# Four norms between sublayers: the second 1/RMS applied to the products' results instead of their operand

## The chip, the cores and the metric

The kernel runs on one core of a Trainium2 chip. The metric is the device time of one execution in microseconds: the median of several runs. A profile of one execution shows what each engine did: TensorE (PE, with its weight loads as PEld), VectorE (DVE), ScalarE (ACT), GpSimd (POOL) and SyncE (SP), which here only issues the weights' DMAs.

## The reference, cut to what matters

Two blocks of a hybrid model over 256 tokens and 16 learned ones (T = 272), width 1024. In the first block two layers follow each other, a gated delta rule and an mLSTM, each with a convolving FFN behind it, and a norm on both sides of every sublayer ("sandwich"):

```python
for i in range(DEPTH):                      # 2 layers
    a_in = rms_norm(hs, norm_w[i, 0])
    mix = gated_deltanet(a_in, ...) if i % 2 == 0 else mlstm(a_in, ...)
    hs = hs + keep * rms_norm(mix, norm_w[i, 1])
    f = conv_ffn(rms_norm(hs, norm_w[i, 2]), ...)
    hs = hs + keep * rms_norm(f, norm_w[i, 3])
...
# conv_ffn: u = causal_depthwise_conv(h @ w_up, conv_w) + conv_b
#           (silu(u[..., :2816]) * u[..., 2816:]) @ w_down
x = x + 0.5 * swiglu(rmsnorm(x, ffn1_norm), ffn1_w_gu, ffn1_w_down)   # second block begins
```

So a sublayer's result goes through one norm (first 1/RMS) into the residual, and the new residual through another (second 1/RMS) into the next sublayer's first products. This happens four times: delta rule to FFN, FFN to mLSTM, mLSTM to FFN, FFN to the second block's SwiGLU.

## The kernel before

**Operands.** Activations lie with features on the partitions, 8 tiles of 128 features by T, S + 2 = 258 or S = 256 tokens. Every product is made in three passes of fp32r: activations and weights are split into a high part (ScalarE's copy) and a low part (source minus high part, on VectorE or GpSimd), and TensorE adds high*high, low*high and high*low. `wload` (line 356) brings a block of at most 1024 weight values a partition (512 KB) by a DMA on SP's queue, three buffers deep, and makes its high part (`wh`) on ScalarE and its low part (`wl`) on VectorE, or in two pieces on GpSimd. Which of the two is set by tables: `POOL_FIRST` (0, 4, 2, 2, 0, 0, 0) is how many loads behind each norm go to GpSimd first, `POOL_EVERY` (0, 0, 0, 2, 4, 0, 4) says that later every so many do. Both are indexed by `seg`, which counts norms.

**Products.** `linears_g` makes the first two products behind a norm together (gate and up, or q and k, 256 columns each), operand tile by operand tile as these come; its four results take three of the ring's buffers in PSUM and the bank pc2. `linear_g` makes 256 columns: two result tiles in two of three PSUM buffers. `conv_ffn` has eleven blocks of 256 gate and 256 up columns; for each result its `conv` takes one ScalarE step and two VectorE steps that read PSUM. `swiglu_up` has eleven blocks without a convolution.

**The norm.** While the last products of a sublayer run, `mix_tile` takes each result tile: ScalarE squares it (`macc`), multiplies it by the norm's weight into `mw` and squares that (`mwacc`), VectorE multiplies `mw` by the residual (`mcross`). TensorE adds these over the partitions (`early` the first parts, `colsum_end` the last). `mix_end` works out the first 1/RMS `r`, and from the three sums the new residual's sum of squares `c` and the second 1/RMS `r2`. The residual's update, mw times r and hst plus mw, runs on GpSimd; then, for each operand tile, VectorE makes y = residual * weight * r2 (`xn`), ScalarE the high part, VectorE the low part (`xhl`). At T = 272 `warm` gives TensorE some products whose result nobody reads while it waits.

**Order.** One pass over the program writes the instructions; `Threads` interleaves generators (the main thread, the mLSTM's gates and heads, the memory's products) into one fixed order of TensorE's queue by an estimate of all engines' times. Within `manual_schedule` VectorE and GpSimd run in the order of the text. Behind the second norm `ml_gates` multiplies 8 gate columns, turns the result to tokens on the partitions and works out running sums that all four heads wait for. `add_tile` adds the SwiGLU's result to the residual (`ps * 0.5 + x`), and `prenorm` is the fifth norm, which this change doesn't restructure; between these the memory's products fill TensorE's waits.

## Time and profile before

| | us |
|---|---|
| median of 3 runs | 1698.15 (1695.23 to 1698.38) |
| span of the profiled execution | 1697.1 |
| TensorE busy | 1568.4 (92%) |
| VectorE busy | 1096.0 (65%) |
| ScalarE busy | 924.7 (54%) |
| GpSimd busy | 633.7 (37%) |

The profile comes from one execution. The share of busy time is a mean over stages with different limits; what a stage is worth is read from its own stretch. In a timeline a line gives start, length, engine, operation and tiles, and in brackets how long the engine sat idle before it and what ended that.

### The profile page before, as it was taken

How to read it: one execution, taken by the hardware profiler on the slowest of the kernel's cores; microseconds unless marked ns; L12 is line 12 of the kernel's file. 1: busy time of each engine (PE TensorE's matmuls, PEld its weight loads, DVE VectorE, ACT ScalarE, POOL GpSimd, SP SyncE). 2: the span in 40 equal slices, each digit the busy share in tenths (PEclk: the TensorE clock that was granted, in tenths of full speed). 3: DMA queues.
4: the chain of work that ended last, by engine and by line, in shares of the span. 5: the costliest groups of instructions: out<-in, count | busy, mean ns of one | idle time of the engine just before them, and what ended most of it. 6: DMA issues, size and time to landing. Idle time of an engine off the chain costs nothing.

```text
span 1697.1 us, 31097 instructions
## 1 busy us (share of the span) xinstructions
PE 1568.4 (92%) x11949; PEld 1475.9 (87%) x11949; DVE 1096.0 (65%) x2118; ACT 924.7 (54%) x1877; POOL 633.7 (37%) x585
## 2 busy tenths in 40 slices
PE   7888888899799997999799998999997999999999
PEld 5778787799799996888799997999986789989987
DVE  3888877767788757357777667545459563465543
ACT  3567767655466553446466555544444664554442
POOL 3675554330500004551544443212265548512221
PEclk7999999999999999899999998999998999999999
DMA  4322221226355552345366553656554335546564
GB/s 120 105 83 62 76 63 51 76 88 214 91 179 169 171 177 76 103 112 161 100 184 188 180 173 120 199 171 195 172 168 125 114 92 155 177 148 186 181 192 149
DMA packets 238570, 235.45 MB, mean 139 GB/s; under 512 B 11254, under 2 KB 226054, under 8 KB 238422
## 3 DMA queue, kind: packets, MB, share of 16 engines
q1 hardware_dynamic: 237318, 230.87, 45.4%
q0 software_dynamic: 832, 2.28, 0.5%
q8 instruction: 94, 1.54, 0.4%
q14 instruction: 54, 0.44, 0.1%
q10 hardware_dynamic: 272, 0.31, 0.1%
HBM read 232.39 MB, written 1.05 MB: 138 GB/s over the span
## 4 chain that ended last, share of the span: by engine, by line
PE 67%; DVE 22%; ACT 5%; DMA 3%; issue 2%; POOL 1%; ACTq 0%; DVEq 0%; POOLq 0%
PE ps L191 52%; PE pst L191 4%; DVE rq_a L191 3%; DVE cy L191 3%; DVE RT L191 2%; ACT wh L191 2%; DVE rq_y L191 1%; DVE wl L191 1%; POOL wl L378 1%; DMA wraw<-in_ffn_w_up_dram 1%; DVE xhl L191 1%; PE xp L191 1%; DVE xn L191 1%; DVE fy L191 1%; DVE on L191 1%
## 5 line engine op out<-in xcount | busy, mean ns | idle before, releaser
L191 PE MATMUL ps<-xhl,wh 128*128 128x256 f32 (+2 forms) x4624 | 882.0, 293 | 31.9 <-ACT xhl L191 17.3
L191 PEld LDWEIGHTS ps<-xhl,wh 128*128 128x128 f32 x4624 | 721.1, 192 | 42.5 <-ACT xhl L191 19.4
L191 ACT CAST wh<-wraw 128x1024 fp32r<-128x1024 f32 (+2 forms) x436 | 447.8, 1029 | 391.7 <-PE ps L191 263.7
L191 PE MATMUL ps<-xhl,wl 128*128 128x256 f32 (+2 forms) x2312 | 644.3, 288 | 0.8 <-DVE wl L191 0.8
L378 POOL TENSOR_TENSOR wl<-wraw,wh 128x512 fp32r<-128x512 f32 (+3 forms) x264 | 334.3, 1290 | 533.2 <-ACT wh L191 508.9
L191 PEld LDWEIGHTS ps<-xhl,wl 128*128 128x128 f32 x2312 | 435.8, 193 | 1.4 <-DVE wl L191 1.0
L191 DVE TENSOR_TENSOR wl<-wraw,wh 128x1024 fp32r<-128x1024 f32 (+3 forms) x234 | 285.0, 1219 | 210.4 <-ACT wh L191 205.1
L191 POOL TENSOR_TENSOR wl<-wraw,wh 128x512 fp32r<-128x512 f32 (+1 forms) x140 | 180.2, 1309 | 150.6 <-ACT wh L191 138.1
L191 PE MATMUL ps<-hh,wh 128*128 128x256 f32 (+1 forms) x1056 | 191.2, 283 | 0.0
L191 PEld LDWEIGHTS ps<-hh,wh 128*128 128x128 f32 x1056 | 163.4, 189 | 0.0
L191 PE MATMUL ps<-hh,wl 128*128 128x256 f32 (+1 forms) x528 | 149.8, 284 | 0.0
L191 DVE SCALAR_TENSOR_TENSOR fy<-ps,pvt,fy 128x256 f32<-128x256 f32 (+2 forms) x176 | 84.9, 487 | 25.0 <-ACT fy L191 23.1
L191 PEld LDWEIGHTS ps<-hh,wl 128*128 128x128 f32 x528 | 99.7, 189 | 0.0
L191 DVE SCALAR_TENSOR_TENSOR cy<-cx,pvt,cy 128x271 f32<-128x271 f32 (+2 forms) x96 | 73.9, 772 | 9.8 <-ACT cy L191 8.7
L191 DVE TENSOR_TENSOR hh<-fy,hh 128x256 fp32r<-128x256 f32 (+1 forms) x88 | 65.0, 741 | 13.1 <-ACT hh L191 12.8
L191 POOL MEMSET mvt<- 128x4 f32 x4 | 0.4, 102 | 177.2 <-PE ps L191 177.2
L299 POOL TENSOR_TENSOR mw<-mw,rstd 128x544 f32<-128x544 f32 (+5 forms) x20 | 24.1, 1206 | 111.4 <-ACT rstd L191 111.4
L191 ACT ACTIVATE fy<-ps,pvt 128x272 f32<-128x272 f32 (+1 forms) x88 | 49.6, 568 | 11.9 <-PE ps L191 11.3
L191 PE MATMUL pst<-wh,hh 128*128 128x512 f32 x176 | 55.0, 394 | 0.0
L191 ACT CAST hh<-fy 128x256 fp32r<-128x256 f32 (+1 forms) x88 | 35.6, 407 | 30.3 <-DVE fy L191 29.7
L191 DVE CAST_PREDICATED RT<-lvl,w 128x512 f16<-128x512 uint8 x67 | 44.9, 682 | 6.0 <-PE w L191 5.3
L191 PE MATMUL ps<-og,wh 128*128 128x272 f32 x256 | 48.6, 289 | 0.2 <-DVE og L191 0.2
(511 smaller groups left out, 2369.8 us busy)
## 6 DMA issues: line engine op xcount, KB each, us to landing
wraw<-in_ffn_w_up_dram SPq DMA_DIRECT2D x88, 512.0 KB
wraw<-in_ffn_w_gu_dram SPq DMA_DIRECT2D x88, 512.0 KB
wraw<-in_ffn_w_down_dram SPq DMA_DIRECT2D x79, 512.0 KB
wraw<-in_gdn_w_in_dram SPq DMA_DIRECT2D x48, 512.0 KB
wraw<-in_w_in_dram SPq DMA_DIRECT2D x41, 512.0 KB
wraw<-in_ml_w_in_dram SPq DMA_DIRECT2D x24, 512.0 KB
wraw<-in_gdn_w_out_dram SPq DMA_DIRECT2D x16, 512.0 KB
wraw<-in_ml_w_out_dram SPq DMA_DIRECT2D x8, 512.0 KB
```

The costliest lines, as they stand in the source:

```text
L191: r = f(*args, **kw)
L299: (eng or self.V).tensor_tensor(out, a, b, op)
L378: eng.tensor_tensor(l[:, a, b], r[:, a, b], h[:, a, b].bitcast(F32), ALU.subtract)
```

## The change

Behind the four norms the residual's update moves from GpSimd to VectorE. As soon as a residual tile is updated, its product with the norm's weight, not yet times r2, is split into high and low part (`raw`), and the first products take it. The sum of squares and r2 are worked out in between and behind; r2 is kept as `self.r` and multiplies results:

- `conv_ffn`: for the first three of eleven blocks every result is multiplied by r2 into SBUF (`scaled`) ahead of the convolution. Meanwhile `scaled_operand` makes the operand as before, a few tiles behind each product; the other blocks take it.
- `mlstm`: q and k of the first two heads and v of heads 0 and 1 take r2 when they leave PSUM, on VectorE instead of ScalarE; the gates take it by tokens, for which r2 is transposed.
- the second block's SwiGLU: the gate's results are scaled in all eleven blocks, and the factor of up is applied behind the down product, in `add_tile`, as two steps.

Further: of the early sums only `macc`'s remains early; the late weight's low part is set to VectorE; `warm` runs five products once instead of two and seven. Comments and docstrings are taken out too.

```diff
@@ mix_tile
-            self.th.add([self.early([self.macc, self.mwacc, self.mcross], N)])
+            self.th.add([self.early([self.macc], N)])
@@ mix_end
         pm = yield from self.colsum_end(0, self.macc[1])
-        pb = yield from self.colsum_end(1, self.mwacc[1])
-        pa = yield from self.colsum_end(2, self.mcross[1])
+        pb = yield from self.colsum(self.mwacc, N, "pc1")
+        yield ["pc2"]
+        pa = yield from self.colsum(self.mcross, N, "pc2")
...
-            self.rstd(r2[:], c, D, NW[1])
-            for k in range(0, KD, 2):
-                y = [self.sm(N, "xn", "y") for _ in range(2)]
-                for n in range(2):
-                    self.stt(y[n][:], src[k + n], self.pv(wcol + k + n), r2[:], ALU.mult, ALU.mult)
-                    self.A.copy(X[k + n][0], y[n][:])
-                for n in range(2):
-                    self.tt(X[k + n][1], y[n][:], X[k + n][0].bitcast(F32), ALU.subtract)
...
+                self.tt(w, w, r[:, None, :].to_broadcast([128, n, N]), ALU.mult)
+                if k == 1:
+                    self.tt(u[:], pb[:], r[:], ALU.mult)
+                    self.stt(u[:], pa[:], 2.0, u[:], ALU.mult, ALU.add)
+                self.tt(s2, s2, w, ALU.add)
+                for j in range(k, k + n):
+                    h, l = raw[j]
+                    wc = self.pv(wcol + j)
+                    self.act(h, src[j], AF.Copy, scale=wc)
+                    self.stt(l, src[j], wc, h.bitcast(F32), ALU.mult, ALU.subtract)
                 if k == 2:
+                    self.prefetch(loads[late:], low, self.V)
                     for f in low:
                         f()
+                    self.tt(u[:], u[:], r[:], ALU.mult)
+                    self.tt(c, u[:], c, ALU.add)
+            self.near_load = self.nload + POOL_FIRST[self.seg]
+            self.rstd(r2[:], c, D, NW[1])
+        return raw, self.scaled_operand(src, wcol, N) if full else None
+
+    def scaled_operand(self, src, wcol, N):
+        X = []
+        for k, (h, l) in enumerate(self.xslots(N)):
+            y = self.sm(N, "xn", "y")
+            self.stt(y[:], src[k], self.pv(wcol + k), self.r[:], ALU.mult, ALU.mult)
+            self.split(h, l, y[:])
+            X.append((h, l))
+            yield X
+
+    def scaled(self, p, N):
+        y = self.sm(N, "py")
+        self.tt(y[:], p, self.r[:], ALU.mult)
+        return y[:]
@@ conv_ffn
-                y = conv(p, 2 * c + m)
+                y = conv(self.scaled(p, N) if c < 3 else p, 2 * c + m)
...
-                yield from self.linear_g(W, c * 256, 256, KD, X, N, gate)
-                yield from self.linear_g(W, FF + c * 256, 256, KD, X, N, up)
+                for c0, fn in ((c * 256, gate), (FF + c * 256, up)):
+                    yield from self.linear_g(W, c0, 256, KD, x, N, fn)
+                    if len(X) < KD:
+                        X = next(todo) and next(todo)
@@ ml_gates
+        yield [self.r[:], "pb1"]
+        p = self.bank("pb1", (128, 3, 128), "mrp")
+        for t, (o, P) in enumerate(TT):
+            self.tr(p[:P, t, :], self.r[:, o:o + P])
+        rt = self.cst([128, 3], name="rtok", tag="rtok")
+        for t, (o, P) in enumerate(TT):
+            self.V.tensor_copy(rt[:P, t:t + 1], p[:P, t, 0:1])
...
-            self.V.tensor_copy(ga[:P, t, :], p[:P, t, :])
+            self.ts(ga[:P, t, :], p[:P, t, :], rt[:P, t:t + 1], ALU.mult)
@@ mlstm
+                elif (kind, n) in raws:
+                    self.stt(t[:, m, :], p, sc, self.r[:], ALU.mult, ALU.mult)
@@ swiglu_up
-                self.act(gs[m][:], p, AF.Silu)
+                self.act(gs[m][:], self.scaled(p, S) if late else p, AF.Silu)
@@ add_tile
-        self.stt(x, ps, scale, x, ALU.mult, ALU.add)
+        if scale == 0.5:
+            y = self.sm(S, "ady", "y")
+            self.stt(y[:], ps, scale, self.r[:], ALU.mult, ALU.mult)
+            self.tt(x, x, y[:], ALU.add)
```

## Rows read from the trace of the kernel before

**Rows 1.** The page's first lines: span, and TensorE's busy time, its share and its instructions.

```profile
span 1697.1 us, 31097 instructions
...
PE 1568.4 (92%) x11949; PEld 1475.9 (87%) x11949; DVE 1096.0 (65%) x2118; ACT 924.7 (54%) x1877; POOL 633.7 (37%) x585
```

**Rows 2.** Windows around the four norms: busy us of each engine (instructions), granted clock, DMA.

```profile
425.20:454.90 29.70, 22.45 (x129) 19.85 (x128) 21.70 (x30) 12.15 (x22) 18.38 (x15) 0.89 0.18 55
643.90:676.00 32.10, 24.11 (x142) 20.11 (x140) 23.03 (x35) 13.16 (x26) 15.49 (x13) 0.89 0.13 35
809.35:837.06 27.71, 21.27 (x126) 19.19 (x127) 19.66 (x29) 10.81 (x19) 17.06 (x15) 0.88 0.16 51
1021.24:1052.50 31.26, 24.78 (x134) 22.38 (x133) 22.04 (x41) 15.36 (x40) 16.29 (x14) 0.84 0.28 85
```

**Rows 3.** Chain of work at the first norm, 425 to 456 us: start, us, what.

```profile
427.09 0.49 ACT rstd L191
...
436.29 2.86 DVE xn L191 x2
...
440.71 6.30 PE ps L191 x38
...
449.38 1.90 DVE xhl L191 x2
```

**Rows 4.** Timeline, VectorE, 426 to 447 us: start, us, operation, [idle before it <- releaser].

```profile
428.07 0.44 DVE L191 TENSOR_TENSOR sqn<-rsp,rstd 128x272 f32<-128x272 f32 x1 [1.56 <-ACT rstd L191]
...
429.10 0.91 DVE L191 TENSOR_TENSOR sqn<-sqn,rstd 128x272 f32<-128x272 f32 x1
...
440.93 0.90 DVE L191 SCALAR_TENSOR_TENSOR xn<-hst,pvt,rstd 128x272 f32<-128x272 f32 x2
...
442.68 1.22 DVE L191 TENSOR_TENSOR wl<-wraw,wh 128x1024 fp32r<-128x1024 f32 x1
```

**Rows 5.** Timeline of the other engines at the first norm, 425 to 452 us.

```profile
426.06 0.43 ACT L191 ACTIVATE sq<-mw 128x272 f32<-128x272 f32 x1
...
426.43 1.08 PE L191 MATMUL rsp<-sq,ones 128*128 128x272 f32 x4
...
447.03 2.00 ACT L191 CAST wh<-wraw 128x1024 fp32r<-128x1024 f32 x2 [1.86 <-PE ps L191]
...
448.16 5.50 POOL L378 TENSOR_TENSOR wl<-wraw,wh 128x512 fp32r<-128x512 f32 x4 [7.80 <-ACT wh L191]
```

**Rows 6.** Tile fy, first FFN, 450 to 640 us: duration ns min/median/max.

```profile
L191 DVE SCALAR_TENSOR_TENSOR fy<-ps,pvt,fy x88: 486/496/502, 452.4 to 580.8; 128x271 f32<-128x271 f32 x44, 128x270 f32<-128x270 f32 x44
...
L191 DVE TENSOR_TENSOR fy<-fy,sg x22: 431/442/1529, 458.1 to 581.3; 128x272 f32<-128x272 f32 x22
```

**Rows 7.** Tile fy, second FFN, 830 to 1015 us.

```profile
L191 DVE SCALAR_TENSOR_TENSOR fy<-ps,pvt,fy x88: 468/479/485, 834.6 to 961.8; 128x256 f32<-128x256 f32 x88
...
L191 DVE TENSOR_TENSOR fy<-fy,sg x22: 410/738/1515, 841.3 to 962.3; 128x256 f32<-128x256 f32 x22
```

**Rows 8.** Windows: second and third 256 columns of both FFNs' up-projections.

```profile
454.90:480.10 25.20, 23.71 (x190) 23.53 (x189) 20.82 (x32) 16.67 (x28) 4.25 (x4) 1.00 0.61 187
837.10:862.00 24.90, 23.28 (x194) 23.10 (x193) 18.65 (x30) 16.27 (x28) 11.58 (x10) 1.00 0.61 188
```

**Rows 9.** Timeline behind the second norm, 666 to 690 us: the mLSTM's gates.

```profile
668.03 0.38 ACT L191 COPY gr<-psmg 8x272 f32<-8x272 f32 x1 [2.40 <-PE psmg L191]
...
669.77 0.30 DVE L191 COPY mga<-mgp 128x8 f32<-128x8 f32 x3 [3.67 <-PE mgp L191]
...
672.42 1.26 DVE L191 TENSOR_SCALAR lp_s<-lp_t 128x12 f32<-128x12 f32 x1 [1.66 <-ACT lp_t L191]
...
681.32 0.59 PE L191 MATMUL mbp<-mlf,cc 128*128 128x4 f32 x2 [5.34 <-DVE mlf L191]
```

**Rows 10.** Timeline behind the fifth norm, 1236 to 1244 us.

```profile
1236.58 0.42 DVE L191 SCALAR_TENSOR_TENSOR hst<-ps,hst 128x256 f32<-128x256 f32 x1 [5.75 <-PE ps L191]
...
1243.24 0.30 PE L191 MATMUL krp<-xhl,wh 128*32 128x256 f32 x1 [0.29 <-ACT memv L191]
```

More of the change, by code (lines that the diff above doesn't have):

```diff
@@ L353, in log1p_exp_neg_abs, with wload @@
         return p
-    def wload(self, w, k0, nk, c0, nc_, pieces=1, late=None, own=None):
+    def wload(self, w, k0, nk, c0, nc_, pieces=1, late=None, own=None, eng=None):
         key = w.tensor.name, k0, c0
@@ L679, in warm, with mix_end @@
             self.mm(p[:, :x.shape[1]], self.ones[:], x)
-    def mix_end(self, src, wcol, N, loads=(), late=1):
+    def mix_end(self, src, wcol, N, loads=(), late=1, full=True):
         late = len(loads) - late
@@ L1609, in mlstm @@
         self.lane = None
-        yield from self.linears_g([job("q", 0), job("k", 0)], KD, X, T)
+        yield from self.linears_g([job("q", 0), job("k", 0)], KD, raw, T)
+        X = next(todo) and next(todo)
         for kind, n in (("v", 0), ("v", 1), ("q", 1), ("k", 1), ("v", 2), ("v", 3), ("o", 0), ("o", 1), ("o", 2), ("o", 3)):
@@ L1615, in mlstm @@
             else:
-                yield from self.linear_g(w, c0, 256, KD, X, T, fn)
+                yield from self.linear_g(w, c0, 256, KD, raw if (kind, n) in raws else X, T, fn)
+                while len(X) < KD:
+                    next(todo)
+                    if len(X) in (5, 8):
+                        break
         return Y
@@ L1669, in first @@
         self.pause[1].set()
-        X = yield from self.mix_end(hs, PV_F1, S, self.ffn_loads(i["ffn1_w_gu_2"][0]))
+        X, _ = yield from self.mix_end(hs, PV_F1, S, self.ffn_loads(i["ffn1_w_gu_2"][0]), full=False)
         self.x2 = hs
```

67 lines of the change are left out of this document (33 added, 34 removed).

## The prediction

> **What bounds the kernel now.** I read the page's first lines, then the stretches around the norms, then the chain and the timelines inside them. TensorE is busy for 92% of the span [rows 1], so time is won only where it waits. One kind of such place is the norm behind each sublayer: from the last product of a sublayer to the end of the two products that follow (gate and up, or q and k) there pass 29.70, 32.10, 27.71 and 31.26 us, in which TensorE is busy 22.45, 24.11, 21.27 and 24.78 us, part of it at the lower clock (mean granted 0.84 to 0.89) or with work put in to fill time [rows 2]. The reader should see why it lasts in the chain of the first one [rows 3]: sums and the first 1/RMS (its Ln starts at 427.09, VectorE uses the result at 428.07 [rows 4]), then a second 1/RMS, and only at 436.29 the first scaled operand. VectorE's small steps are slow there: the operation with one operand in PSUM takes 0.44 us, the next, with both in SBUF, 0.91 [rows 4], while GpSimd updates the residual. Later the operands 6 and 7 wait behind two weight casts of 2.00 us on ScalarE [rows 5] and end at about 451.3 [rows 3].
>
> **The new way to the first products.** The first norm is worked out; the others are scaled from it.
> Sums: two of the three early sums no longer stand ahead of the one that the first 1/RMS needs. ScalarE's last own square ends at 426.49 [rows 5], and Ln started at 427.09 [rows 3]: up to 0.6 saved, so 1/RMS is usable 2.3 us behind the last product instead of 2.87.
> Operands: the second 1/RMS leaves the path; the residual's update comes onto it, from GpSimd to VectorE. A dependent VectorE step costs about 0.52 (two from 428.07 to 429.10), one that multiplies and subtracts 0.45 (0.90 for two), a weight's low part 1.22 [rows 4]. No row shows the 544-wide step on VectorE: between 0.65 (by elements from the 1.22) and 0.88 (two of 0.44), I take 0.75, near the middle, as it is as close to one bound as to the other. Operand 0: 0.52 + 0.52 + a ScalarE copy of 0.5 + 0.45 = 2.0. Operand 1 with two steps of the second sum in between: 2.9. Each of three pairs: 0.75 + 0.75 + 0.5 + 0.45 + 0.45 = 2.9, together 8.7. Between them the late weight's low part and two more steps of the sum, 2.2. Together 15.8 us.
> A new collision: TensorE has used up operands 0 to 3 while VectorE still makes 4 to 7, so the next two weights are cast then and GpSimd makes their low parts, four pieces in 5.50 us [rows 5], against VectorE. Between 0 and 5.5 us; I take 2.2, as the loop's steps that are left then are about half in number of those that GpSimd's pieces could hold.
> Behind the last operand 26 products remain at 0.125 (23.71 us for 190 [rows 8]), 3.25.
> Sum: 2.3 + 15.8 + 2.2 + 3.25 = 23.55 against 29.70, 6.1 us earlier. Third norm, 258 wide (15.0 for 15.8): 22.75 against 27.71, 5.0 earlier. Second, with 0.4 for the gates' products in between: 23.95 against 32.10, 8.1 earlier. Fourth: no GpSimd pieces (VectorE makes these low parts, behind the second 1/RMS): 2.3 + 14.9 + 1.8 + 1.2 + 2.9 = 23.1 against 31.26, 8.2 earlier; the memory's products that fill the wait now are still done beside it. TensorE starts each time some 8 us earlier than today, but VectorE paces it, so the start isn't the gain.
>
> **What takes it back behind the norms.** First and third norm (the two convolving FFNs): for three of eleven column blocks every result is first scaled by VectorE, 12 times 0.44, and the scaled operand is made after all, 8 times 0.45 + 0.43: 12.3 us more (11.8 in the second FFN). In the two blocks behind the first, VectorE is idle for 25.20 - 20.82 = 4.4 us and 24.90 - 18.65 = 6.25 us [rows 8]. It can begin on results when the second 1/RMS is done, 22.1 us into the stretch (15.8 + 2.3 + 2.2 + four steps of 0.45), at 447.3 instead of 452.4 [rows 6], 5.1 earlier; in the second FFN at 830.65 instead of 834.6 [rows 7], 4.0 earlier. Short: 12.3 - 4.4 - 5.1 = 2.8 and 11.8 - 6.25 - 4.0 = 1.55 us.
> The convolution's steps now read the scaled copy in SBUF, not PSUM. From PSUM none of the 88 took over 0.502 us, while the product with both operands in SBUF takes 0.44 in the median and up to 1.53 in the first FFN [rows 6], and 0.74 in the median in the second [rows 7], where GpSimd makes half the low parts (11.58 us busy in these two blocks, against 4.25 [rows 8]). Bounds for what this adds: nothing, or one operation held by about 1.0 us for each of GpSimd's pieces, 4 in the first FFN (two more weights behind the four pieces counted above) and 10 in the second [rows 8]. I take 2 and 4.5, half and nearly half, as the medians 0.44 and 0.74 say that holding follows GpSimd's share. Below nothing it can't be, as no SBUF operation becomes a PSUM one.
> The Trainium skill's page "SBUF — State Buffer", section "Who interferes with whom", has a rule against this edit: a VectorE instruction with two SBUF inputs contends with a GpSimd instruction that reads SBUF, one with a single SBUF input doesn't. By that rule all 24 convolution steps of the three blocks become exposed, and the sum would go to the upper bound, 14 us instead of 6.5; the trace agrees in kind (0.502 at most, against 1.53).
> TensorE bears some lateness: the last pair's convolution and products lie behind the stretch, and one result buffer in three is spare, about 24 matmuls or 2.9 us; an estimate of 4 us (0 to 6). So the first FFN ends its third block at +2.8 + 2 - 4 = 0.8 us later than today, the second at 1.55 + 4.5 - 4 = 2.0 later: the 6.1 and 5.0 are spent there.
> Second norm: TensorE stands at 676 and waits for the gates' sums until 681.32, and the steps of their chain are held by GpSimd too (1.26 us for 12 columns) [rows 9]. The gates' product ends with operand 7, some 3.5 us sooner than the 668.0 of [rows 9], but 1/RMS must be transposed and copied in the same bank (about 1.3 us), and VectorE's queue gets four result scalings and two operands (3.5 us) among the 11.5 us of steps from 669.77 to 681.3. So that wait ends between 3 us earlier and 2 later; I take 0.5 earlier. The longer chain lets the planner put some 16 products (2 us) ahead of the wait. Together 2.5 of the 8.1 stay. If that cover is not used, 0.5.
> Fourth norm: VectorE only gets 22 scalings of gate results (9 us over 130), with room; I let 8.2 stand. At the end of that FFN each of 8 tiles takes two VectorE steps instead of one of 0.42; the last is on the path to the fifth norm, where TensorE waits just 0.29 us today [rows 10] behind the memory's products: 0.4 lost.
> ScalarE's eight more copies per norm lie in its idle time (12.15 of 29.70 us busy [rows 2]); SP issues the same loads, earlier.
>
> **Sum.** 0.8 - 2.5 + 2.0 - 8.2 + 0.4 = -7.5 us. The profiled execution's span is 1697.1 us, its median of runs 1698.15, 1.05 above; -7.5 gives 1689.6 in the span and 1690.6 us as the median.
>
> **Rivals.**
> VectorE keeps up: holding is small and the lateness is borne, so the 6.1, 5.0 and 8.1 stay in full. 1698.15 - 27.4 + 0.4 = 1671 us; half of it, 1681. For it: operations from PSUM were never slowed; the steady blocks of the first FFN run TensorE at full with VectorE at 83% (20.82 of 25.20). Against: the shortfall above.
> Second 1/RMS late: GpSimd holds the loop by the full 5.5 instead of 2.2, so at the first three norms the results leave 3.3 us later, which isn't made up: up to 6.6 of the 7.5 gone in the FFNs, 1697 us, no change.
> VectorE bound (slower): in blocks 0 to 2 of both FFNs each GpSimd piece holds an operation, 14 at 1.0 instead of the 6.5 counted, 7.5 us more, and TensorE bears no lateness, 8 more: 1706 us (1702 to 1710). It decides once 11 of these 15.5 us are paid. For it: the median of 0.74 [rows 7], and that the shortfall leaves no idle time to absorb a hold; against: TensorE's waits there are one of 1.5 us per FFN today (25.20 - 23.71 [rows 8]). The rule of the Trainium skill named above leads to this case.
> That it doesn't do what it says is small: the scaling is plain, and no gain rests on a clock.
>
> **How the numbers follow.** The likeliest case 0.5, 1690.6 (1684 to 1697); VectorE keeps up 0.2, 1671 to 1684; 1/RMS late 0.12, 1697; VectorE bound 0.18, 1706. The range leaves out the outer part of the second and of the last: 1674 to 1705 us. A difference of 0.2%, 3.4 us, is about what measuring can tell from none. Faster by more: 0.45 of the likeliest's 0.5, 0.2 of the second, some of the third: 0.67. Within: 0.15. Slower: 0.18.
>
> **What would show it.** Right: the four stretches shrink to about 23 us, TensorE's first product there follows 1/RMS by under 2 us, VectorE's busy share in the two blocks behind rises above 95%, and TensorE gets new waits for VectorE (scaled results, low parts) of 4 to 7 us per FFN. The whole gain should stand behind the fourth norm. Wrong: blocks 1 and 2 of an FFN in 23.5 us (VectorE kept up), or in over 33 us (bound); the gates' wait behind the second norm gone, or over 8 us; the clock staying at its lower level through the first block.

## The result: 0.6% slower

The changed kernel takes 1707.9 us (median; 1707.3 to 1710.2) against 1698.3 us for the kernel before on the same chip: ratio 1.006, 95% interval 1.0042 to 1.0078. The forecast was 1690.6 us with a range up to 1705; the time is that of the rival that the prediction called "VectorE bound", 1706 (1702 to 1710), though only part of that rival's mechanism came.

The changed kernel's page; the lines answer to [rows 1]:

```profile
span 1705.5 us, 31173 instructions
...
PE 1575.1 (92%) x11936; PEld 1482.6 (87%) x11936; DVE 1131.2 (66%) x2239; ACT 935.7 (55%) x1893; POOL 590.4 (35%) x545
```

VectorE has 35 us more to do, GpSimd 43 us less, TensorE nearly the same, and the span is 8.4 us longer.

The four stretches around the norms in the changed kernel, cut as in [rows 2] (columns as there):

```profile
427.36:454.30 26.94, 21.24 (x121) 19.20 (x120) 19.82 (x33) 11.59 (x22) 8.09 (x6) 0.87 0.26 79
648.67:680.40 31.73, 24.95 (x148) 20.37 (x147) 24.67 (x47) 12.74 (x24) 8.26 (x6) 0.85 0.30 84
811.98:840.27 28.29, 23.05 (x131) 20.76 (x130) 20.28 (x35) 10.84 (x20) 8.05 (x6) 0.82 0.24 78
1031.33:1058.74 27.41, 23.61 (x137) 21.34 (x136) 18.82 (x46) 16.01 (x41) 5.08 (x4) 0.88 0.31 98
```

They last 26.94, 31.73, 28.29 and 27.41 us; 23.55, 23.95, 22.75 and 23.1 were predicted. The third window of [rows 2] starts inside the norm, 1.33 us later behind its first sum product than the other three. Cut like them, that stretch lasts 29.04 us in the kernel before, not 27.71, and the prediction started from a base that was 1.3 us too short there:

```profile
808.02:837.06 29.04, 21.72 (x129) 19.24 (x128) 20.94 (x33) 11.23 (x20) 17.06 (x15) 0.88 0.19 58
```

So the first (29.70 before) and the fourth (31.26) are clearly shorter, the second and third (32.10 and 29.04) by under 1 us. GpSimd's work there is down to about 8 us, and 5 at the fourth; the mean granted clock is lower than before at the first three (0.82 to 0.87) and higher only at the fourth (0.88).

What each part of the program gained or lost can be read off one event that all kernels have: the start of the first sum product at each norm (`rsp<-acc` in TensorE's timeline). In the kernel before these stand at 425.06, 643.76, 807.88, 1021.04 and 1236.38 us, in the changed one at 427.22, 648.53, 811.84, 1031.19 and 1243.08. Against the kernel before the pieces between them changed by

| first to second norm (first FFN) | second to third (mLSTM) | third to fourth (second FFN) | fourth to fifth (SwiGLU) | fifth to the end |
|---|---|---|---|---|
| +2.6 (predicted +0.8) | -0.8 (-2.5) | +6.2 (+2.0) | -3.5 (-8.2) | +1.7 (+0.4) |

The 2.2 us ahead of the first norm are not the change's: the program is the same up to there, and in the experiments this mark lies between 0.6 us earlier and 5.2 later than in the kernel before. In experiments that leave a piece untouched, that piece differs from the kernel before by 0.0 in the first FFN, -1.7 to +0.7 in the mLSTM, -0.7 to -1.3 in the second FFN, -2.1 to +0.8 in the SwiGLU and -1.2 to +0.9 at the end (in one run -4.0), so the second FFN's loss is rather 7 and the SwiGLU's gain rather 3. No piece went in the other direction than predicted, but each came out worse. Between the forecast of -7.5 us and the +8.4 of the profiled span lie 15.9 us: 1.8 and 4.2 in the two FFNs, 4.7 in the SwiGLU, 1.7 in the mLSTM, 1.3 at the end, and the 2.2 ahead of the first norm.

### The profile page after: what moved, and what is told of

It is laid out like the page before. It is cut to its first block, busy times and chain, and to the rows that moved or that the text cites. A ratio compares the mean times of both kernels' runs of the same rounds, so it can differ in the third digit from the quotient of the medians.

```text
span 1705.5 us, 31173 instructions
## 1 busy us (share of the span) xinstructions
PE 1575.1 (92%) x11936; PEld 1482.6 (87%) x11936; DVE 1131.2 (66%) x2239; ACT 935.7 (55%) x1893; POOL 590.4 (35%) x545
## 4 chain that ended last, share of the span: by engine, by line
PE 67%; DVE 22%; ACT 6%; issue 3%; DMA 2%; POOL 1%; ACTq 0%; DVEq 0%; POOLq 0%
PE ps L191 52%; PE pst L191 4%; DVE cy L191 3%; DVE rq_a L191 3%; ACT wh L191 2%; DVE RT L191 2%; DVE fy L191 1%; DVE wl L191 1%; DVE rq_y L191 1%; PE memp L191 1%; POOL wl L382 1%; DVE xn L191 1%; PE xp L191 1%; DVE on L191 1%; DVE xr L191 1%
## 5 line engine op out<-in xcount | busy, mean ns | idle before, releaser
L191 PE MATMUL ps<-xhl,wh 128*128 128x272 f32 (+2 forms) x3408 | 658.7, 293 | 13.5 <-DVE fy L191 3.1
L191 PEld LDWEIGHTS ps<-xhl,wh 128*128 128x128 f32 x3408 | 532.1, 191 | 19.8 <-DVE zs L191 3.4
L191 PE MATMUL ps<-xhl,wl 128*128 128x272 f32 (+2 forms) x1704 | 481.2, 286 | 0.1
L191 PEld LDWEIGHTS ps<-xhl,wl 128*128 128x128 f32 x1704 | 322.7, 191 | 0.3 <-POOL wl L382 0.3
L191 PE MATMUL ps<-xr,wh 128*128 128x256 f32 (+2 forms) x1216 | 231.6, 298 | 23.8 <-ACT xr L191 13.6
L191 PEld LDWEIGHTS ps<-xr,wh 128*128 128x128 f32 x1216 | 196.1, 201 | 28.1 <-ACT xr L191 15.7
L191 PE MATMUL ps<-xr,wl 128*128 128x256 f32 (+2 forms) x608 | 166.4, 296 | 0.8 <-DVE wl L191 0.8
L191 PEld LDWEIGHTS ps<-xr,wl 128*128 128x128 f32 x608 | 116.4, 201 | 1.0 <-DVE wl L191 1.0
L191 DVE SCALAR_TENSOR_TENSOR cy<-cx,pvt,cy 128x271 f32<-128x271 f32 (+2 forms) x96 | 73.9, 773 | 10.6 <-ACT cy L191 9.6
L191 DVE SCALAR_TENSOR_TENSOR fy<-ps,pvt,fy 128x256 f32<-128x256 f32 (+2 forms) x128 | 62.3, 487 | 14.0 <-ACT fy L191 12.6
```

What stands on the lines that cost most here:

```text
L191: r = f(*args, **kw)
```

## Experiments

Every kernel is a version of the changed one, or (`before` in its name) of the kernel before; a norm without the change is left, with what follows it, as in the kernel before. The pieces are set against the profiled run of the kernel before, as above. A kernel's profiled execution lies up to 3.7 us from its median (6.6 in q_before_no_pool), so a piece is good to a microsecond or two.

| kernel | median us (kernel before beside it) | first FFN | mLSTM | second FFN | SwiGLU | end |
|---|---|---|---|---|---|---|
| e1_ffn_only | 1711.1 (1698.5) | +2.9 | -0.4 | +5.6 | -0.9 | +0.2 |
| e2_mlstm_only | 1700.6 (1698.5) | 0.0 | -0.5 | -0.7 | -0.9 | -0.6 |
| e3_swiglu_only | 1697.3 (1698.5) | 0.0 | +0.7 | -1.3 | -4.7 | +1.9 |
| d_ffn_raw_only | 1693.8 (1698.5) | -3.8 | -0.6 | -2.1 | +0.6 | +0.1 |
| f_ffn_no_scaling | 1696.3 (1696.8) | -0.9 | -1.5 | -0.3 | 0.0 | -0.5 |
| g_ffn_pool_memset | 1688.8 (1696.8) | -1.3 | -1.6 | -7.6 | +0.8 | -0.6 |
| g_before_pool_memset | 1692.5 (1696.8) | -2.4 | +0.4 | -3.4 | -0.7 | -0.8 |
| b_swiglu_actorder | 1698.1 (1696.8) | 0.0 | 0.0 | -1.1 | -4.0 | +1.8 |
| p_ffn_no_pool | 1697.2 (1698.4) | -1.3 | +0.5 | +1.3 | -0.5 | +0.9 |
| h_gates_unscaled | 1699.0 (1698.4) | 0.0 | -0.7 | -1.2 | -2.1 | +0.8 |
| n_best | 1713.6 (1698.4) | +10.6 | -0.8 | +9.2 | -4.4 | -0.4 |
| t_after_no_pool | 1699.7 (1697.5) | -1.4 | -0.3 | -0.2 | -0.5 | -0.3 |
| q_before_no_pool | 1696.8 (1697.5) | -0.7 | -1.7 | -3.3 | -0.8 | -4.0 |
| i_mlstm_all_raw | 1695.5 (1697.5) | 0.0 | -3.1 | -1.3 | -1.8 | -1.2 |
| r_three_norms | 1690.0 (1697.5) | -1.3 | -5.3 | -1.2 | -4.5 | -0.6 |
| r_four_norms | 1689.9 (1697.5) | -1.3 | -5.2 | +1.7 | -4.1 | -0.4 |

### Which norm pays

The change at two, one and one of the norms:

```
 SITES = (0, 2)   # e1: ahead of the two convolving FFNs
 SITES = (1,)     # e2: ahead of the mLSTM
 SITES = (3,)     # e3: ahead of the SwiGLU
```

> The change at the first and third norm alone (those ahead of the two convolving FFNs); the other two norms as before. Theory A, 'VectorE bound in the FFNs': set against each other from norm to norm, the changed kernel lost 2.6 us over the first FFN's stretch and 6.2 over the second's, so this kernel takes 8.8 us more than the kernel before: 1707 us (1704 to 1710), ratio 1.005. Rival B, 'the loss needs all four norms' (a later norm that starts in another order of the queues is what pays): well under that, 1698 to 1702 us.

> The change at the second norm alone (ahead of the mLSTM's q, k, v and gates). Theory A: the stretch from the second to the third norm gained 0.8 us in the changed kernel, because the gates' own wait ends about as late as before: 1697.5 us (1696 to 1700). The prediction had 1695.8. Rival B, 'the planner's other order is worth more when only this part moves': 1690 to 1695 us.

> The change at the fourth norm alone (ahead of the SwiGLU, where no second operand is made and every gate and up result takes the factor later). Theory A: gain of 3.45 us up to the fifth norm, 1.7 of it lost behind that: 1696.5 us (1694 to 1699). Rival B, 'the fourth norm pays for the lateness it inherits from the second FFN in the changed kernel' (memory keys and weights that come later against it): alone it gains the predicted 8 us less 0.4, 1690 to 1692 us.

Theory A holds, with the first two kernels 1.1 and 0.6 us above its ranges. The two FFN norms alone cost all of it (ratio 1.0087, 1.0065 to 1.011); the second alone costs nothing or a little (1.0017, 1.0001 to 1.0033), the fourth alone too (1.0, 0.9987 to 1.0013), because 1.9 of its 4.7 us go again behind the fifth norm. The pieces come out much as in the whole changed kernel, so they can be studied one by one.

### Is the new way shorter? Only the raw operand, in all blocks

```
-            x = raw if c < nr else X          # conv_ffn
+            x = raw                           # no scaled operand
-                y = conv(self.scaled(p, N) if c < nr else p, 2 * c + m)
+                y = conv(p, 2 * c + m)        # and the same for the up results
```

> The change at the first and third norm alone, and in the two FFNs behind them all eleven column blocks take the raw operand (kept in the slots of the usual operand), no result is scaled and no scaled operand is made: the second 1/RMS is left out of these two FFNs, so the outputs differ. This keeps the whole way to the first products and takes away VectorE's added work behind it. Theory A, 'VectorE's added work in blocks 0 to 2 gives it back': the gain at the two norms stays, 2.8 us and 2.5 to 5 us, so 1690 to 1693 us, 14 to 17 us under the same kernel with scaling. Rival B, 'the new way itself is no shorter: TensorE waits for the last raw operands at its lower clock': about as the kernel before or slower, 1698 to 1706 us.

1693.8 us, ratio 0.9981 (0.9967 to 0.9994): theory A, 0.8 us above its range. The two FFN pieces are shorter, by 3.8 and 2.1 us, and what is behind the first products runs on undisturbed. The 57 us from the end of the second FFN's first products on, first here, then in e1_ffn_only (columns as in [rows 2]):

```profile
831.30:888.30 57.00, 56.60 (x469) 56.42 (x469) 43.18 (x70) 37.91 (x61) 24.92 (x20) 1.00 0.59 177
```

```profile
840.12:897.12 57.00, 49.69 (x393) 48.89 (x392) 51.56 (x88) 36.67 (x61) 22.46 (x17) 0.97 0.49 148
```

TensorE is busy for 56.60 of 57 us at full clock, against 49.69 at a mean of 0.97, with VectorE at 51.56 instead of 43.18. The difference is the VectorE work that the factor brings.

### Scalings or second operand?

```
-                y = conv(self.scaled(p, N) if c < nr else p, 2 * c + m)
+                y = conv(p, 2 * c + m)        # the operand X is still made
```

> The change at the first and third norm alone, and there the results of the first three column blocks are not scaled (their factor is left out, so the outputs differ): the convolution reads PSUM again, but the scaled operand for the later blocks is still made. VectorE loses, per FFN, 12 scalings of 0.43 us and the holding of 24 convolution steps (0.564 us in the mean where they read the scaled copy in the first FFN, 0.722 in the second, against 0.495 and 0.475 from PSUM): 6.8 and 11.0 us. Theory A, 'what the scaled copies add to VectorE is what gives the gain back': the two FFN stretches turn from +2.9 and +5.6 to -3 and -2, 1693 to 1696 us. Rival B, 'the operand made after all, 16 steps in VectorE's queue between the convolutions, is enough to bind it': they stay above +1 and +3, 1702 to 1706 us.

1696.3 us, ratio 0.9999 (0.9984 to 1.0015): in between, nearer to A. The FFN pieces are -0.9 and -0.3. From e1 to here the scaled copies are worth 3.9 and 5.8 us, from here to the raw operand alone the second operand 2.9 and 1.8. Reading PSUM again, no convolution step is held (VectorE's groups, 833 to 890 us: mean 477 ns of 40):

```profile
L194 DVE SCALAR_TENSOR_TENSOR fy<-ps,pvt,fy 128x256 f32<-128x256 f32 x40 | 18.7, 477 | 5.1 <-ACT fy L194 4.8
```

### Number of steps, or holding by GpSimd?

GpSimd writes zeros where it would read a weight and its high part, in the FFNs of e1_ffn_only and of the kernel before:

```
-                eng.tensor_tensor(l, r, h, ALU.subtract)
+                eng.memset(l, 0.0)            # where eng is GpSimd, in the two FFNs
```

> The change at the first and third norm alone, and in the two FFNs GpSimd writes zeros where it else subtracts the weights' low parts (those low parts are left out, so the outputs differ): GpSimd reads nothing, all of VectorE's steps stay. To be set against the next run, which has the same edit in the kernel before. Theory A, 'GpSimd holds VectorE's steps on two SBUF operands' (24 convolution steps 0.3 us longer and 8 operand steps 0.57 longer in the second FFN, 12 us): the convolution steps from the scaled copy fall to 0.43 us in the mean in both FFNs, and the loss against its control falls from 9 to 2 us or less. Rival B, 'the number of VectorE's steps alone': the loss against its control stays 6 to 9 us, whatever their duration.

> The kernel before with the same edit: in the two FFNs GpSimd writes zeros in place of the weights' low parts (left out, so the outputs differ). It is the control of the run with the change. VectorE is not what TensorE waits for in these FFNs before, so both theories expect 1696 to 1699 us, some 1 us under the kernel before at the most.

1688.8 against 1692.5 us: with GpSimd reading nothing the change at the FFN norms, 12.6 us slower before, is 3.7 us faster than its control. The control is itself 4.3 us faster than the kernel before (0.9975, 0.9961 to 0.9988), where both theories expected 1 us at the most, so GpSimd's subtractions cost that kernel something too, by what they hold or by their length. Against that control the second FFN went from +5.6 to -4.2, the first from +2.9 only to +1.0. VectorE's groups from 833 to 890 us, first with GpSimd's reads (e1_ffn_only), then without (columns: operation, shapes, count | busy us, mean ns of one | idle before; the kernels pass this window at different points, so it is the means that can be compared):

```profile
L194 DVE SCALAR_TENSOR_TENSOR fy<-py,pvt,fy 128x256 f32<-128x256 f32 x24 | 17.1, 722 | 1.9 <-ACT fy L194 1.7
L194 DVE TENSOR_TENSOR wl<-wraw,wh 128x1024 fp32r<-128x1024 f32 x7 | 8.5, 1210 | 0.1
L194 DVE SCALAR_TENSOR_TENSOR xn<-hst,pvt,rstd 128x258 f32<-128x258 f32 x8 | 7.9, 983 | 0.1
```

```profile
L194 DVE SCALAR_TENSOR_TENSOR fy<-py,pvt,fy 128x256 f32<-128x256 f32 x20 | 9.6, 479 | 0.6 <-ACT fy L194 0.4
...
L194 DVE SCALAR_TENSOR_TENSOR xn<-hst,pvt,rstd 128x258 f32<-128x258 f32 x8 | 3.9, 483 | 0.1
```

The convolution step from the scaled copy takes 722 ns in the mean in the one, 479 in the other; the step that makes the second operand 983 and 483. GpSimd still works in the second kernel, but only writes. In the control the product of two SBUF operands, 738 ns in the median in [rows 7], is down to 423 in the mean:

```profile
L194 DVE TENSOR_TENSOR fy<-fy,sg 128x256 f32<-128x256 f32 x10 | 4.2, 423 | 0.3
```

So it is the reads that hold VectorE. The Trainium skill's page "SBUF — State Buffer", section "Who interferes with whom", says just this: an instruction with two SBUF inputs contends with a GpSimd instruction that reads SBUF, not with one that only writes it. These runs agree, and give the price in this kernel: 0.24 us on each of 24 convolution steps and 0.50 on each of 8 operand steps in the second FFN.

In the first FFN rival B holds for what follows the first products: TensorE's two waits for scaled results, in blocks 1 and 3, are as long in the changed kernel (shown first) as without GpSimd's reads (g_ffn_pool_memset), and without the factor (d_ffn_raw_only) neither is there. So these come from the number of VectorE's steps.

```profile
465.04 0.39 PE L191 MATMUL ps<-xr,wh 128*128 128x272 f32 x1 [3.30 <-DVE py L191]
...
486.64 0.52 PE L191 MATMUL ps<-xhl,wh 128*128 128x272 f32 x2 [1.48 <-DVE py L191]
```

```profile
458.37 0.52 PE L194 MATMUL ps<-xr,wh 128*128 128x272 f32 x2 [3.26 <-DVE py L194]
...
479.96 0.52 PE L194 MATMUL ps<-xhl,wh 128*128 128x272 f32 x2 [1.47 <-DVE py L194]
```

What the reads cost the first FFN lies ahead of that: its first products end 26.99 us behind the norm's first sum product in the changed kernel and 23.12 here, and the 3.9 us between them stay the same to the end of the fourth block.

The zeros also make GpSimd faster, so the same was tried with nothing left out, VectorE making those low parts:

```
-POOL_FIRST = (0, 4, 2, 2, 0, 0, 0)
-POOL_EVERY = (0, 0, 0, 2, 4, 0, 4)
+POOL_FIRST = (0, 0, 2, 0, 0, 0, 0)
+POOL_EVERY = (0, 0, 0, 0, 4, 0, 4)
```

> The change at the first and third norm alone, and in the two FFNs VectorE makes every weight's low part, GpSimd none (nothing is left out). GpSimd no longer reads SBUF there, as in the run with the zeros, but VectorE gets its work: 1.22 us for each weight, some four in the first blocks of the first FFN and half of all in the second. Theory A, 'holding costs more than the work': in the second FFN (8 weights in 57 us by GpSimd, 9.8 us of VectorE, for some 13 us of held steps) the stretch falls from +5.6 to +2 to +4 us against the kernel before, and in the first from +2.9 to about +2 to +4; 1702 to 1706 us. Rival B, 'VectorE has no room for them': +7 us or more in the second FFN, 1708 us and above.

> The changed kernel whole, all four norms, with one edit: in the two FFNs VectorE makes the low parts that GpSimd makes (nothing is left out). Theory A, 'the loss of the changed kernel is GpSimd's holding of VectorE's new steps': the two FFN stretches go from +2.6 and +6.2 to the -1.3 and +1.3 of the run with two norms, the rest as in the changed kernel (-0.8, -3.5, +1.7): 11 us less are 1697 us, no loss against the kernel before. Rival B, 'with four norms changed the late second FFN and the memory's work behind it pay in another way': 1702 us or more.

> The kernel before with that same edit, the control: VectorE makes all low parts in the two FFNs. Theory A: TensorE doesn't wait for VectorE there, VectorE is busy 81% in the first FFN's blocks and 74% in the second's, and 8 weights more in 57 us bring it to 90% less the holding that goes; within 3 us of the kernel before, 1695 to 1700 us. Rival B, 'the edit alone is worth as much as it gave the changed kernel': 1686 to 1690 us, and then what the change costs stays 10 us.

With the two FFN norms changed, 1697.2 us (0.9989, 0.9973 to 1.0005) instead of 1711.1; better than theory A expected. With all four, 1699.7 (1.0004, 0.9994 to 1.0015) instead of 1707.9, between the two theories; the SwiGLU's piece gave only 0.5 us in that profile, which stays unexplained. The control can't be told from the kernel before (0.999, 0.9978 to 1.0002); its profiled execution is 6.6 us under its median, so its pieces are not to be trusted to a microsecond. Against this control on the same chip the whole change is still 2.8 us slower (1699.7 against 1696.8), at the edge of what these runs can tell from nothing. That GpSimd's low parts came too late for TensorE is not the cause: in blocks 1 to 3 of the changed kernel's FFNs every wait of TensorE ends with a result of VectorE (`py` or `fy`), none with a weight's part. VectorE's groups of p_ffn_no_pool, same window:

```profile
L194 DVE TENSOR_TENSOR wl<-wraw,wh 128x1024 fp32r<-128x1024 f32 x16 | 19.6, 1224 | 5.4 <-ACT wh L194 5.2
L194 DVE SCALAR_TENSOR_TENSOR fy<-py,pvt,fy 128x256 f32<-128x256 f32 x24 | 11.1, 482 | 0.6 <-ACT fy L194 0.4
```

Sixteen low parts of 1.22 us instead of seven, and still less time in all for the FFN: here what the neighbour held up on a bound engine cost more than doing the neighbour's work. Net of the work that VectorE took over, GpSimd's reading cost e1_ffn_only 13.9 us by the medians (8.5 by its two FFN pieces) and the whole changed kernel 8.2.

### What is in the way behind the second norm

```
-            self.ts(ga[:P, t, :], p[:P, t, :], rt[:P, t:t + 1], ALU.mult)
+            self.V.tensor_copy(ga[:P, t, :], p[:P, t, :])   # h: and no transposed 1/RMS
```

> The change at the second norm alone, without the factor on the mLSTM's gates: no transposition of 1/RMS and no product with it (the factor is left out of the gates, so the outputs differ); q, k and v take it as before. With it TensorE waited 2.9 us for the transposed 1/RMS and 4.5 us for the gates' sums. Theory A, 'the gain at the second norm goes into the gates' path': the stretch to the third norm gains 2 to 4 us instead of 0.5, 1695 to 1697 us. Rival B, 'it goes into the late scaling of q, k and v and the raw loop': it stays at 0 to 1 us, 1698 to 1700 us.

Theory A fell: 1699.0 us, the piece at -0.7. The wait for the transposed 1/RMS went, but the gates' sums made TensorE wait for 10.0 us instead of 4.5 (first e2_mlstm_only, then this kernel, TensorE's timeline):

```profile
691.14 0.59 PE L194 MATMUL mbp<-mlf,cc 128*128 128x4 f32 x2 [4.50 <-DVE mlf L194]
```

```profile
686.33 0.59 PE L194 MATMUL mbp<-mlf,cc 128*128 128x4 f32 x2 [9.99 <-DVE mlf L194]
```

The sums start 42.80 us behind the norm's first sum product in the one and 40.83 in the other, against 37.56 before. What delays their chain stands between its links in VectorE's queue (e2_mlstm_only):

```profile
674.16 2.93 DVE L194 SCALAR_TENSOR_TENSOR xn<-hst,pvt,rstd 128x272 f32<-128x272 f32 x2
...
681.37 0.16 DVE L194 TENSOR_TENSOR mga<-mga,mgb 128x24 f32<-128x24 f32 x1
682.39 3.46 DVE L194 TENSOR_TENSOR xhl<-xn,xhl 128x272 fp32r<-128x272 f32 x4 [0.86 <-ACT xhl L194]
685.77 0.17 DVE L194 TENSOR_SCALAR mga<-mga 128x24 f32<-128x24 f32 x1
```

Between two links of 0.16 us (`mga`, at 681.37 and 685.77) lie four of the scaled operand's low parts, held, 3.46 us. So that operand was taken away, without leaving anything out: q, k, v and o all take the raw one, and VectorE scales all 24 results.

```
-        raws = ("q", 0), ("k", 0), ("v", 0), ("v", 1)
+        raws = [(kind, n) for kind in "qkvo" for n in range(4)]   # and X = raw
```

> The change at the second norm alone, but no scaled operand is made there: q, k, v and o all take the raw operand (kept in the slots of the usual one), and each of their 24 results takes the factor (nothing is left out). This takes 16 operand steps, several held by GpSimd, out of VectorE's queue ahead of the gates' chain, whose sums TensorE waited for 4.5 us, 42.8 us into the stretch, against 37.6 in the kernel before. Theory A, 'the operand made after all stands in the gates' way': the sums come at 37 to 39 us, and the stretch to the third norm gains 2 to 4 us instead of 0.5: 1695 to 1697 us. Rival B, 'the gain is lost elsewhere (the transposition, the results' scalings, lower clock)': 0 to 1 us, 1698 us or more.

1695.5 us, ratio 0.9985 (0.9972 to 0.9999), the piece at -3.1: theory A. The sums start 37.03 us behind the first sum product:

```profile
683.94 0.59 PE L194 MATMUL mbp<-mlf,cc 128*128 128x4 f32 x2 [4.35 <-DVE mlf L194]
```

### The fourth norm and ScalarE's order

```
-        with self.tc.manual_schedule(engines={mybir.EngineType.DVE}):
+        with self.tc.manual_schedule(engines={mybir.EngineType.DVE, mybir.EngineType.Activation}):
```

> The change at the fourth norm alone, and ScalarE is held to the written order within the loop of raw operands, as VectorE is already: the copies for operands 4 to 7 stand ahead of the second 1/RMS and are no longer split by it. Theory A, 'the loop is delayed by what ScalarE does in between' (1.98 us for the memory's keys ahead of operand 2, 2 us of weight casts and a logarithm ahead of operands 4 and 5): 1 to 2 us less than with the change at the fourth norm alone, 1694 to 1696.5 us. Rival B, 'the last operand's VectorE steps set the end anyway': no difference, 1697 us.

No gain: 1698.1 us (1.0005, 0.9994 to 1.0017), the piece at -4.0 against -4.7. The order fixed there binds the loop's own steps to one another; what stands between them stayed. In ScalarE's timeline of e3_swiglu_only the memory's keys (`memkt`) come ahead of operands 2 and 3 (`xr`, 1032.75) and two weight casts ahead of 4 and 5 (1038.51):

```profile
1031.05 0.59 ACT L194 COPY memkt<-memp 128x512 f32<-128x512 f32 x1 [1.60 <-PE memp L194]
...
1032.75 0.89 ACT L194 ACTIVATE xr<-hst,pvt 128x256 fp32r<-128x256 f32 x2
...
1036.20 1.99 ACT L194 CAST wh<-wraw 128x1024 fp32r<-128x1024 f32 x2 [0.80 <-PE ps L194]
...
1038.51 0.89 ACT L194 ACTIVATE xr<-hst,pvt 128x256 fp32r<-128x256 f32 x2
```

What is left as the cause is the foreign work in ScalarE's queue; it is not shown, as no run took it away.

### Versions that were to beat both

```
 SITES = (0, 2, 3)                       # n_best; and ScalarE's order as above
-        nr = 3 if todo else 0
+        nr = 1 if todo else 0           # scaled operand in one go ahead of block 1
-                self.tt(y[:], p, gs[m][:], ALU.mult)               # SwiGLU, up
+                self.tt(y[:], self.scaled(p, S) if late else p, gs[m][:], ALU.mult)
```

> What the runs so far point to, nothing left out: the second norm as before; at the first and third the raw operand for the first column block alone (4 scalings instead of 12, then the scaled operand); at the fourth the whole change, but the up results take the factor at once, so no tile at the end of that FFN takes two steps; ScalarE held to the written order in the loop of raw operands. Theory A, by the runs (each result scaling taken away, and each held step with it, gives back a share of the 3.9 and 5.8 us that all twelve cost; the operand costs 2.9 and 1.8): first FFN -1 to +1, second -1 to +2, SwiGLU -4 to -5, behind the fifth norm +0.5 instead of +1.9: 1692 to 1697 us, at or a little under the kernel before. Rival B, 'the operand, now made in one go ahead of the second block, is what binds': FFNs +3 each, 1699 to 1702 us.

Rival B, and worse than it said: 1713.6 us (1.0084, 1.0062 to 1.0107). VectorE's queue had the first block's held convolutions (four steps 3.33 to 3.37 us) ahead of the second operand, and TensorE stood still for one wait of 9.1 us in the first FFN:

```profile
462.96 0.60 PE L194 MATMUL ps<-xhl,wh 128*128 128x272 f32 x1 [9.11 <-ACT xhl L194]
```

Its SwiGLU edit, however, works: the loss behind the fifth norm went from +1.9 to -0.4.

```
 SITES = (0, 1, 3)      # r_three_norms; (0, 1, 2, 3) in r_four_norms
```

The last two join what had helped: no GpSimd reads in the FFNs, no second operand behind the second norm, the up results scaled at once; at three norms, and with the third as the fourth:

> What the runs point to, nothing left out: the change at the first, second and fourth norm; VectorE makes all low parts in the two FFNs; behind the second norm all products take the raw operand and no scaled one is made; in the SwiGLU the up results take the factor at once. By the segments measured so far: first FFN -1.3, mLSTM -3.1, SwiGLU and behind it -3 to -4.8, second FFN 0 to -2: 1687 to 1692 us. If the segments don't add up (the third norm's and the SwiGLU's order changes with what comes before): 1693 to 1697 us.

> The same with the change at the third norm too. Theory A, 'without GpSimd's reads the second FFN is left with VectorE's number of steps, which cost what the shorter way gains': 0 to 3 us more than with three norms, 1689 to 1694 us. Rival B, 'with the holding gone the third norm gains its predicted 2 to 5 us': 1683 to 1688 us.

Both are faster than both kernels: 1690.0 us (0.9953, 0.9938 to 0.9968) and 1689.9 (0.9959, 0.9943 to 0.9974). The third norm still gives nothing: the second FFN's piece is 2.9 us longer with it in the profiles, and the medians are the same. The mLSTM's piece is -5.3 and -5.2 in these two where i_mlstm_all_raw had -3.1; the 2 us more are not explained.

## Why the prediction was wrong, step by step

Two terms failed most. The holding in the second FFN stood at 4.5 us and measured 9.6. The gain at the fourth norm stood at 8.2 us; 4.2 came by the end of its first products, and 3.5 in its piece. Then the lateness that TensorE was to bear stood at 4 us per FFN and was 1.7 in the first, and the second and fifth norm fell short by 1.7 and 1.3 us.

**The raw loop.** Its single costs were right: the 544-wide step takes 0.72 us (0.75 assumed), a pair of low parts 0.92 (0.90), the first factor is used 2.24 us behind the last product (2.3). Wrong was what lies between them. VectorE's timeline of the changed kernel at the first norm, and below it the same place without GpSimd (p_ffn_no_pool):

```profile
442.56 2.22 DVE L191 SCALAR_TENSOR_TENSOR xr<-hst,pvt,xr 128x272 fp32r<-128x272 f32 x2 [1.99 <-ACT xr L191]
444.71 1.79 DVE L191 TENSOR_TENSOR mw<-mw,rstd 128x544 f32<-128x544 f32 x1
...
447.84 0.92 DVE L191 SCALAR_TENSOR_TENSOR xr<-hst,pvt,xr 128x272 fp32r<-128x272 f32 x2 [0.59 <-ACT xr L191]
...
451.68 3.38 DVE L191 SCALAR_TENSOR_TENSOR fy<-py,pvt,fy 128x271 f32<-128x271 f32 x4 [0.51 <-ACT fy L191]
```

```profile
439.36 2.54 DVE L194 TENSOR_TENSOR wl<-wraw,wh 128x1024 fp32r<-128x1024 f32 x2
441.82 0.91 DVE L194 SCALAR_TENSOR_TENSOR xr<-hst,pvt,xr 128x272 fp32r<-128x272 f32 x2
442.64 0.72 DVE L194 TENSOR_TENSOR mw<-mw,rstd 128x544 f32<-128x544 f32 x1
```

GpSimd and ScalarE in the changed kernel at that time:

```profile
440.56 5.36 POOL L382 TENSOR_TENSOR wl<-wraw,wh 128x512 fp32r<-128x512 f32 x4 [71.04 <-ACT wh L191]
```

```profile
439.38 1.05 ACT L191 CAST wh<-wraw 128x1024 fp32r<-128x1024 f32 x1 [2.70 <-PE ps L191]
440.33 0.52 ACT L191 ACTIVATE rstd<-ssq,epst 128x272 f32<-128x272 f32 x1
440.76 1.03 ACT L191 CAST wh<-wraw 128x1024 fp32r<-128x1024 f32 x1
441.69 0.42 ACT L191 ACTIVATE rstd<-rstd 128x272 f32<-128x272 f32 x1
442.02 0.92 ACT L191 ACTIVATE xr<-hst,pvt 128x272 fp32r<-128x272 f32 x2
```

The pair at 442.56 takes 2.22 instead of 0.91 us and the step at 444.71 1.79 instead of 0.72: GpSimd holds the loop for 2.4 us, and 2.2 was assumed. But ahead of that pair VectorE idles for 1.99 us for ScalarE (0.59 at the other pairs), whose copies of operands 4 and 5 stand behind two weight casts and the second 1/RMS's logarithm and exponential. The prediction let the copies "lie in its idle time" at no cost beyond their own 0.5: it had counted ScalarE's load (12.15 of 29.70 us), not its order. Without GpSimd, VectorE makes two low parts in that gap (439.36).

**The 26 products behind the last operand** were priced at 0.125 us each, 3.25 together. From that operand's end (448.76) to the end of the stretch (454.30) 5.5 us passed: TensorE was still at the products ahead of them until 449.39, and the 26 took 4.7. TensorE had waited 3.0 and 2.2 us for operands, and its clock was below full (third number from the end of the line: granted clock). The changed kernel, and below it p_ffn_no_pool, where the first of these waits came (2.99 us) and the second was 0.18:

```profile
448.00:454.00 6.00, 6.00 (x36) 6.00 (x37) 5.32 (x10) 2.29 (x4) 2.73 (x2) 0.72 0.16 55
```

```profile
448.00:454.00 6.00, 6.00 (x50) 6.00 (x49) 5.47 (x11) 5.25 (x8) 0.00 (x0) 1.00 0.36 98
```

At 0.72 over six microseconds, part of it is at 1.2 GHz. In p_ffn_no_pool the 26 take the 3.25 us that were priced. The prediction had named the clock as what would make it wrong, and had no term for it.

Together: the loop from the first factor's use to the last operand took 19.15 us for the forecast 18.0 (1.5 more idle time for ScalarE than the 0.5 counted, 0.2 more holding, 0.5 less in the other steps), and what is behind it 5.5 for 3.25. That makes the 3.4 us by which the first stretch was missed (26.94 for 23.55). Without GpSimd's reads (p_ffn_no_pool) the first products end 23.5 us behind the first sum product, against 29.8 before and 27.0 in the changed kernel: the predicted 6 us, for a partly different reason.

**Blocks 0 to 2.** The prediction added a shortfall of VectorE (2.8 us in the first FFN, 1.55 in the second) and the holding (2 and 4.5), and took off 4 us of lateness that TensorE was to bear. All three can be read. VectorE's last product of the third block (its sixth `fy<-fy,sg`), first FFN before and changed, then second FFN before and changed:

```profile
484.03 0.44 DVE L191 TENSOR_TENSOR fy<-fy,sg 128x272 f32<-128x272 f32 x1
```

```profile
490.60 0.44 DVE L191 TENSOR_TENSOR fy<-fy,sg 128x272 f32<-128x272 f32 x1
```

```profile
865.53 0.42 DVE L191 TENSOR_TENSOR fy<-fy,sg 128x256 f32<-128x256 f32 x1
```

```profile
879.82 0.41 DVE L191 TENSOR_TENSOR fy<-fy,sg 128x256 f32<-128x256 f32 x1
```

Counted from each norm's first sum product, VectorE is done 4.4 us later than before in the first FFN and 10.3 in the second; 4.8 and 6.05 were forecast. Of this the held convolution steps are 1.6 and 5.6 us (what the 24 steps take over their median; 2 and 4.5 were forecast), and held operand steps another 4.0 in the second FFN (8 steps of 0.97 us in the mean instead of 0.47), for which the prediction had nothing, though they too read two SBUF operands. The rest, 2.8 and 0.7, is the shortfall. The fourth block's first result is cast on ScalarE (`hh<-fy`) 71.56 us behind the first sum product, 68.90 before, and 74.17 in the second FFN, 67.17 before: 2.7 and 7.0 us late, where 0.8 and 2.0 were forecast. (In the first FFN the third block's products end 0.9 us late, as forecast; the wait of 1.48 us in the fourth, shown above, comes on top.) So TensorE bore 1.7 and 3.3 us of VectorE's lateness.

In the first FFN the lateness that TensorE was to bear is therefore the step that failed. Without GpSimd's reads (g_ffn_pool_memset, p_ffn_no_pool) VectorE is 0.5 us late there and TensorE 1.2 to 1.3 early, and again 1.7 to 1.8 us are borne; no row had shown the 4. In the second FFN it is the holding, 9.6 us where 4.5 stood, most of the difference in the operand steps. The tile `fy` in the two FFNs, for [rows 6] and [rows 7]:

```profile
L191 DVE SCALAR_TENSOR_TENSOR fy<-py,pvt,fy x24: 489/496/1523, 451.7 to 489.0; 128x271 f32<-128x271 f32 x12, 128x270 f32<-128x270 f32 x12
...
L191 DVE TENSOR_TENSOR fy<-fy,sg x22: 427/442/444, 459.7 to 586.1; 128x272 f32<-128x272 f32 x22
```

```profile
L191 DVE SCALAR_TENSOR_TENSOR fy<-py,pvt,fy x24: 467/475/1520, 837.8 to 878.0; 128x256 f32<-128x256 f32 x24
```

What is held in an FFN is now the convolution (up to 1.52 us) and, in the first, no longer the product behind it (1.53 us before, now 0.444): the hold falls here on whatever step with two SBUF operands is due when GpSimd reads. The convolutions were held for 7.3 us in both FFNs together, near the 6.5 that was taken and half of the bound of 14; with the operand steps it is 11.2. The rule of the Trainium skill named there was right on which steps are held, and it covers the operand steps too.

Of the signs that the prediction set down, TensorE's new waits came: 11.3 us in five waits for scaled results in both FFNs together, within the 4 to 7 per FFN. Blocks 1 and 2 took 29.5 and 30.5 us, between its two signs (23.5 and 33), with VectorE busy for 89% and 97% of them.

**Second norm.** 2.5 was to stay of 8.1, with the gates' wait as the cover; 0.8 stayed. The prediction had the queue right ("four result scalings and two operands") but counted two operands where all 16 operand steps stood in VectorE's queue ahead of the chain's last links, part of them held, and TensorE waited 2.9 us for the transposed 1/RMS, for which 1.3 us of work had been counted. What came is near its lower end, 0.5, and within what untouched pieces differ by.

**Fourth norm.** 8.2 was predicted. To the end of the first products the changed kernel is 4.2 us shorter, and 6.3 with this norm alone (25.16 against 31.49 us); 3 to 5 were kept. The memory's work, which the prediction said is "still done beside it", is on ScalarE's and VectorE's queues inside the loop. The sum for this norm was scaled from the first and not worked out for its own neighbours. How much each of them costs stays open.

**Fifth norm.** 0.4 was predicted for one more VectorE step. The step adds two SBUF operands, and GpSimd was at the near weights' low parts (e3_swiglu_only):

```profile
1231.77 5.21 POOL L385 TENSOR_TENSOR wl<-wraw,wh 128x512 fp32r<-128x512 f32 x4 [2.53 <-ACT wh L194]
...
1233.29 1.30 DVE L194 TENSOR_TENSOR hst<-hst,ady 128x256 f32<-128x256 f32 x1
```

The step takes 1.30 us, where 0.4 had been counted; TensorE's first product there came 0.7 us later than before. The rest of the 1.7 lies in small waits further on and was not traced.

**The rivals.** "VectorE bound" came in its place, the FFNs, and in kind: held steps, and lateness not borne in full. That its time came is in part luck. It counted 15.5 us more in the FFNs, and their pieces came out 6.0 us above the forecast: 11.2 us of holding instead of its 14, and 5 of the 8 us of lateness borne instead of none. The rest came where it changes nothing: 7.7 us in the mLSTM, the SwiGLU and the end, and 2.2 ahead of the first norm. It had 0.18, and the likeliest case 0.5, because the operand steps' holding was left out and the lateness stood at 4 us without a row that showed it.

## What to carry to other kernels

Moving a factor from an operand to the results moves work to the engine that empties PSUM; the question is then how busy that engine is in the blocks right behind, with every step counted that the factor turns from a PSUM reader into a reader of two SBUF operands. If another engine reads SBUF beside such steps, count the held time as work of the engine that is held, at full price, and try giving it the other engine's work. Look at the order of each helper's queue between the steps of a chain, not at its share of busy time.

## What the runs showed that was not expected

In the two FFNs GpSimd's low parts, taken as a relief of VectorE, cost more than having VectorE make them: e1_ffn_only fell from 1711.1 to 1697.2 us when VectorE took them over. In the kernel before the same edit gave nothing that can be measured (1696.8 against 1697.5). GpSimd instructions that only write held nothing: 479 ns beside them, 722 beside those that read. After waits of 3.0 and 2.2 us TensorE's granted clock was 0.72 from 448 to 454 us, and 26 products took 4.7 us there; after the first of these waits alone they took 3.25.
